# Keeping the instruction scheduler's time by a simulated timeline of the engines instead of plain estimates


## The chip, the cores and the metric

The kernel runs on one core of one Trainium2 chip. The metric is the device time of one execution in microseconds (us). The engines named below are TensorE (PE, matrix products), VectorE (DVE), ScalarE (ACT), GpSimd (POOL, which does nothing but fills of constants in this kernel) and SyncE (SP), whose queue issues most DMA transfers. Each engine runs its own list of instructions in the order in which the list was written, and an instruction that waits holds up those behind it in its list.

## The reference, cut to what matters

Two blocks of a language model are chained over 512 tokens of width 1024, all in fp32. The first block has a mixer of gated convolution and block-sparse attention, a gated MLP, a mixer with a linear recurrence, and a second MLP. The second block puts 16 learned tokens ahead of the 512 and has two layers, each with a hybrid mixer and a convolution-gated MLP:

```
def hybrid_mixer(...):
    proj = n @ w_in
    aq, ak, av, az, aa, ab, bq, bk, bv, iq, ik, iw = jnp.split(proj, SPLIT_POINTS, axis=-1)
    o_a = gated_deltanet(aq, ak, av, az, aa, ab, conv_a, a_log, dt_bias, a_out_norm)
    o_b = dsa_attention(bq, bk, bv, iq, ik, iw, q_norm, k_norm, kidx_norm, cos_a, sin_a, cos_i, sin_i)
    gates = jax.nn.sigmoid(n @ w_gate + b_gate).reshape(Bsz, T, 2, D)
    y = gates[:, :, 0] * (o_a @ w_branch_a) + gates[:, :, 1] * (o_b @ w_branch_b)
    return y @ w_out

def gated_deltanet(...):
    ...
    lhs = m + jnp.eye(CHUNK, dtype=f32)
    sol = lax.linalg.triangular_solve(lhs, rhs, left_side=True, lower=True, unit_diagonal=True)
    ...
    def step(S, inp):
        v_new = u_c - jnp.einsum('bhcd,bhde->bhce', w_c, S)
        o = (jnp.einsum('bhcd,bhde->bhce', q_c * jnp.exp(g_c)[..., None], S)
             + jnp.einsum('bhcs,bhse->bhce', qk_c, v_new))
        S = S * jnp.exp(g_last) + ...
        return S, o
```

The attention (`dsa_attention`) scores every key for every query with a small indexer, keeps the best keys and attends to those. The delta net solves a unit lower triangular system for each chunk of 128 tokens and carries a state `S` from chunk to chunk.

## The kernel before

**Products.** Every large matrix product runs in split precision: weight and activation are each cut into a high and a low part, and `products` (matmuls in line 146) forms high·high, high·low and low·high for each of 8 blocks of 128 rows, in two column halves. One block of 128 output columns is so 48 matmuls of 258 or 264 columns. Each weight block is loaded by an SP transfer into `wraw` (3 buffers), cast to its high part `whi` on ACT (line 97), and the low part `wlo` is subtracted on DVE (line 98; two buffers each). Product tiles `mm` in PSUM have two buffers, and so has each of the tags `a`, `b` and `c` that all smaller matmuls write to.

**The mixer of the second block** (`mixer_2`, run for layer 0 from about 1120 us and for layer 1 from about 2040 us) is where small work is laid between products. It goes through these stages: the norm's broadcast of the inverse root to all partitions (matmul of line 279, of a diagonal that DVE writes in line 266); products for queries and keys with the sums of squares (line 765) and the indexer's scores (lines 876 and 877); 12 products for the delta net's convolved inputs, with the selection of keys and the attention (lines 1014 to 1070) beside them; and 4 + 16 products for `z` and the gates (`w_gate`), with the delta net's matrices (`dn_keys`, `dn_prep`) beside them. Closures in the list `fill` are run between products in program order, one list entry per product:

```
            for k, p in enumerate(prods):
                if k < len(steps):
                    self.fill.append((1, lambda k=k: [f() for f in steps[k]]))
                p()
```

**The triangular solve** (`dn_solve`) is a chain over engines and transfers. The last `dn_prep` matmuls (line 1186) and DVE products (line 1188) give the matrices; SP stores them to DRAM (`md`, line 1191) and loads them in another layout (`U`, line 1220); 31 steps of two DVE instructions follow (lines 1226 and 1228), a copy (line 1229), SP stores and loads again (`xz`, lines 1232 to 1240), and then four rounds of small matmuls join the blocks: `pair1` (line 1250) to `pair4` (line 1283), each with a copy by ACT behind it. After that the state recurrence runs over 5 tiles of tokens: `dn_read` (line 1330), `dn_u` (line 1338), `dn_write` (line 1348) and `dn_out` (lines 1360 and 1364). The products with `w_branch_b` (line 1444, 8 blocks of 24 matmuls) don't need the delta net, those with `w_branch_a` do.

**What sets the order.** The kernel is written in one program order; the tile framework's scheduler then runs that program in a model of time and puts on each engine's list, whenever that engine is free in the model, the waiting instruction with the best priority. Its notion of how long things take thus decides which instruction stands ahead of which on an engine. The lists are fixed before the run. The line that the change touches is 1679, where the framework's context is opened around `body`, which writes the whole kernel.

## Time and profile before

| what | value |
|---|---|
| median of 3 runs | 2968.08 us (2965.66 to 2968.27) |
| profiled execution | 2972.7 us, of which the span of its profile 2970.9 us |
| PE busy in the span | 97% |
| mean granted TensorE clock | 0.974 of full |

The span runs from the first to the last profiled instruction. PE, PEld, DVE, ACT and POOL are engines (PEld is TensorE's loading of weights, which runs beside its matmuls). PEclk is the clock that TensorE was granted; its two levels are 2.4 GHz (1.00) and 1.2 GHz (0.50), and a value between the two is a mix over the stretch.

### The profile page before, as it was taken

How to read it: one execution, taken by the hardware profiler on the slowest of the kernel's cores; microseconds unless marked ns; L12 is line 12 of the kernel's file. 1: busy time of each engine (PE TensorE's matmuls, PEld its weight loads, DVE VectorE, ACT ScalarE, POOL GpSimd, SP SyncE). 2: the span in 40 equal slices, each digit the busy share in tenths (PEclk: the TensorE clock that was granted, in tenths of full speed). 3: DMA queues.
4: the chain of work that ended last, by engine and by line, in shares of the span. 5: the costliest groups of instructions: out<-in, count | busy, mean ns of one | idle time of the engine just before them, and what ended most of it. 6: DMA issues, size and time to landing. Idle time of an engine off the chain costs nothing.

```text
span 2970.9 us, 44580 instructions
## 1 busy us (share of the span) xinstructions
PE 2878.1 (97%) x18009; PEld 2521.7 (85%) x18009; DVE 1856.1 (62%) x3462; ACT 1047.0 (35%) x1939; POOL 14.2 (0%) x117
## 2 busy tenths in 40 slices
PE   7999999999999999998999999999999999999999
PEld 5767888876788887888999999999788999998897
DVE  7886535458653557698757554555788757565553
ACT  3444212245321233353633332223444634322222
POOL 0000000000000000000000000000000000000000
PEclk9999999999999999898999999999998999999999
DMA  4213333332333333121355232324221354332333
GB/s 124 63 32 120 92 100 92 94 98 71 93 94 98 93 99 111 54 65 51 102 137 154 83 89 86 93 84 122 57 65 43 86 141 116 109 90 85 103 88 90
DMA packets 509860, 272.23 MB, mean 92 GB/s; under 512 B 40112, under 2 KB 494918, under 8 KB 509398
## 3 DMA queue, kind: packets, MB, share of 16 engines
q1 hardware_dynamic: 493520, 245.24, 29.2%
q10 hardware_dynamic: 16134, 24.14, 2.5%
q8 instruction: 142, 2.33, 0.3%
q14 instruction: 64, 0.52, 0.1%
HBM read 249.11 MB, written 20.23 MB: 91 GB/s over the span
## 4 chain that ended last, share of the span: by engine, by line
PE 87%; DVE 8%; DMA 2%; ACT 2%; issue 1%; SPq 0%; ACTq 0%; DVEq 0%
PE mm L146 74%; PE mm L1444 2%; DVE wlo L98 1%; PE b L1065 1%; PE b L765 1%; PE a L393 1%; PE a L877 1%; PE c L418 1%; PE a L1022 1%; PE b L1062 1%; DVE ac L704 1%; DVE m L994 1%; DVE ac L966 1%; DVE selw L996 0%; PE a L876 0%
## 5 line engine op out<-in xcount | busy, mean ns | idle before, releaser
L97 ACT CAST whi<-wraw 128x1024 fp32r<-128x1024 f32 (+1 forms) x472 | 458.3, 971 | 1412.1 <-PE mm L146 1179.9
L146 PE MATMUL mm<-xh,whi 128*128 128x264 f32 (+2 forms) x3376 | 898.4, 323 | 15.4 <-ACT whi L97 6.4
L146 PE MATMUL mm<-xh,wlo 128*128 128x264 f32 (+2 forms) x3376 | 892.4, 322 | 11.6 <-DVE wlo L98 11.6
L146 PE MATMUL mm<-xl,whi 128*128 128x264 f32 (+2 forms) x3376 | 893.0, 322 | 0.0
L98 DVE TENSOR_TENSOR wlo<-wraw,whi 128x1024 fp32r<-128x1024 f32 (+1 forms) x472 | 529.2, 1121 | 423.1 <-ACT whi L97 413.2
L146 PEld LDWEIGHTS mm<-xh,whi 128*128 128x128 f32 x3376 | 564.8, 191 | 71.2 <-ACT whi L97 7.2
L146 PEld LDWEIGHTS mm<-xh,wlo 128*128 128x128 f32 x3376 | 566.6, 191 | 65.4 <-DVE wlo L98 16.7
L146 PEld LDWEIGHTS mm<-xl,whi 128*128 128x128 f32 x3376 | 563.1, 191 | 50.8 <-issue 7.0
L146 PE MATMUL mm<-hh,whi 128*128 128x512 f32 (+1 forms) x1040 | 340.7, 355 | 0.0
L146 PE MATMUL mm<-hh,wlo 128*128 128x512 f32 (+1 forms) x1040 | 340.4, 355 | 0.0
L146 PE MATMUL mm<-hl,whi 128*128 128x512 f32 (+1 forms) x1040 | 339.5, 354 | 0.0
L146 PEld LDWEIGHTS mm<-hh,wlo 128*128 128x128 f32 x1040 | 184.0, 188 | 27.7
L146 PEld LDWEIGHTS mm<-hl,whi 128*128 128x128 f32 x1040 | 183.8, 188 | 27.8
L146 PEld LDWEIGHTS mm<-hh,whi 128*128 128x128 f32 x1040 | 184.0, 188 | 26.5
L502 DVE TENSOR_TENSOR down<-mm,r 128x512 f32<-128x512 f32 x32 | 22.1, 692 | 106.7 <-PE mm L146 106.7
L361 DVE SCALAR_TENSOR_TENSOR val<-z,cw,val 128x512 f32<-128x512 f32 x120 | 84.8, 746 | 0.5
L1496 DVE TENSOR_TENSOR fx<-mm,rbc 128x528 f32<-128x528 f32 (+1 forms) x44 | 30.7, 702 | 81.6 <-PE mm L146 81.6
L1509 DVE TENSOR_TENSOR fc<-fc,mm 128x528 f32<-128x528 f32 (+1 forms) x44 | 30.6, 696 | 76.5 <-PE mm L146 76.5
L146 PE MATMUL mm<-qkv,whi 128*128 128x264 f32 (+1 forms) x384 | 67.4, 284 | 0.0
L1501 DVE SCALAR_TENSOR_TENSOR fc<-fx,vcols,fc 128x528 f32<-128x528 f32 (+1 forms) x88 | 66.2, 758 | 1.4
L1097 DVE TENSOR_TENSOR ac<-mm,rbc 128x528 f32<-128x528 f32 (+1 forms) x32 | 22.4, 700 | 70.3 <-PE mm L146 70.1
L1444 PE MATMUL mm<-xh,whi 128*128 128x264 f32 (+1 forms) x256 | 54.7, 295 | 7.3 <-DVE ax L1458 6.1
(538 smaller groups left out, 3327.5 us busy)
## 6 DMA issues: line engine op xcount, KB each, us to landing
wraw<-in_w_up SPq DMA_DIRECT2D x152, 512.0 KB, 4.0
wraw<-in_w_down SPq DMA_DIRECT2D x96, 512.0 KB, 4.3
wraw<-in_w_in SPq DMA_DIRECT2D x52, 512.0 KB, 3.9
wraw<-in_w_gate SPq DMA_DIRECT2D x32, 512.0 KB, 4.2
wraw<-in_ab_w_in SPq DMA_DIRECT2D x20, 512.0 KB, 3.7
wraw<-in_c_w_in SPq DMA_DIRECT2D x16, 512.0 KB, 3.9
wraw<-in_w_out SPq DMA_DIRECT2D x16, 512.0 KB, 5.4
wraw<-in_w_down SPq DMA_DIRECT2D x32, 192.0 KB, 2.6
```

The source lines that it names most:

```text
L97: self.S.copy(hi[:, :n], raw[:, :n])
L98: self.V.tensor_tensor(lo[:, :n], raw[:, :n], hi[:, :n].bitcast(F32), op=ALU.subtract)
L146: ins = self.PE.matmul(o, lhsT=wt[:, k % chunk, :], rhs=xt[:, t0:t1], start=n == 0, stop=n == 3 * kb - 1)
L361: V.scalar_tensor_tensor(cacc[b], z[b][:, j:j + S], w, cacc[b], op0=ALU.mult, op1=ALU.add)
L393: PE.matmul(ps[:, :W], lhsT=qk[p][r0:r0 + 64, P * i:P * i + P], rhs=qk[4 + p][r0:r0 + 64, :W], start=True, stop=True)
L418: PE.matmul(po[:, 64 * j:64 * j + 64], lhsT=pts[:, P * c:P * c + P], rhs=vt[c][:, h:h + 64], start=c == 0, stop=c == i)
L704: self.V.tensor_tensor(t[o], raw[i], tab[1][i], op=ALU.mult)
L765: PE.matmul(p5[:n, i:i + 1], lhsT=q[:, t0:t0 + n], rhs=self.ones[:, 0:1], start=True, stop=True)
L1444: PE.matmul(o, lhsT=wt[:, k, :], rhs=xt[:, m0 + t0:m0 + t1], start=k == 0 and j == 0, stop=k == 3 and j == 2)
L1496: V.tensor_tensor(self.v3(x[:, 2:2 + TG], TG), ps, self.v3(self.rbc, TG), op=ALU.mult)
L1501: V.scalar_tensor_tensor(c, x[:, d + j:TG + j], w(j), c, op0=ALU.mult, op1=ALU.add)
L1509: V.tensor_tensor(self.v3(c, TD), self.v3(c, TD), ps, op=ALU.mult)
```

## The change

The scheduler's clock is changed: it takes the time of instructions from a simulated timeline of the engines and no longer from plain per-instruction estimates. No instruction's computation is changed. GpSimd does memsets alone before and after.

```
-    with tile.TileContext(nc) as tc:
+    with tile.TileContext(nc, schedule_with_timeline_sim=True) as tc:
         body(tc, a, out)
```

The MLPs, the output products and nearly all of the first block's recurrence mixer keep their order. Instructions move in the first block's first mixer and in both hybrid mixers. In the rows below, a name is a tile and a number its instance: `mm` a product's tile, `xh`, `xl` and `whi`, `wlo` the parts of activation and weight, `a` and `b` small PSUM tiles, and the sizes at the end are of the output; x2 stands for two column halves.

Where layer 0's hybrid mixer begins, PE's list of before has the norm's broadcast (line 279) after 4 matmuls of the second product:

```order
L146 MATMUL mm_8390<-xl_1428_7544,whi_8392 128x264 x2
L146 MATMUL mm_8390<-xh_1427_7543,wlo_8393 128x264 x2
L146 MATMUL mm_8462<-xh_1413_7529,whi_8464 128x264 x2
L146 MATMUL mm_8462<-xl_1414_7530,whi_8464 128x264 x2
L279 MATMUL a_8355<-diag_8314,ones 128x512
L285 MATMUL a_8359<-diagm_8316,ones 128x16
L810 MATMUL mm_8539<-xh_1413_7529,whi_8533 80x264 x2
L810 MATMUL mm_8539<-xl_1414_7530,whi_8533 80x264 x2
L279 MATMUL a_8445<-diag_8375,ones 128x512
```

After the change the same broadcast (`a_8355`) stands in a later product:

```order
L146 MATMUL mm_8706<-xh_1421_7537,wlo_8709 128x264 x2
L146 MATMUL mm_8706<-xh_1423_7539,whi_8708 128x264 x2
L146 MATMUL mm_8706<-xl_1424_7540,whi_8708 128x264 x2
L279 MATMUL a_8355<-diag_8314,ones 128x512
L285 MATMUL a_8359<-diagm_8316,ones 128x16
L146 MATMUL mm_8706<-xh_1423_7539,wlo_8709 128x264 x2
L146 MATMUL mm_8706<-xh_1425_7541,whi_8708 128x264 x2
L146 MATMUL mm_8706<-xl_1426_7542,whi_8708 128x264 x2
```

The broadcast, and with it what waits for it, has moved behind 174 further product matmuls.

At the first small matmuls behind the triangular solve of layer 0 (`pair1`, line 1250), PE's list of before goes on with gate products (`mm_12235` is one of `w_gate`):

```order
L146 MATMUL mm_12128<-xh_1427_7543,whi_12130 128x264 x2
L146 MATMUL mm_12128<-xl_1428_7544,whi_12130 128x264 x2
L146 MATMUL mm_12128<-xh_1427_7543,wlo_12131 128x264 x2
L1250 MATMUL a_12183<-qkv_2099_11637,dec_11088 32x32
L1250 MATMUL b_12195<-qkv_2099_11637,dec_11198 32x32
L146 MATMUL mm_12235<-xh_1413_7529,whi_12237 128x264 x2
L146 MATMUL mm_12235<-xl_1414_7530,whi_12237 128x264 x2
L146 MATMUL mm_12235<-xh_1413_7529,wlo_12238 128x264 x2
```

After the change `pair1` stands behind all gate products and behind the first two `w_branch_b` products (line 1444):

```order
L1444 MATMUL mm_13064<-xh_2222_12625,whi_13057 128x264 x2
L1444 MATMUL mm_13029<-xl_2223_12626,whi_13022 128x264 x2
L1444 MATMUL mm_13029<-xh_2222_12625,wlo_13023 128x264 x2
L1444 MATMUL mm_13064<-xl_2223_12626,whi_13057 128x264 x2
L1444 MATMUL mm_13064<-xh_2222_12625,wlo_13058 128x264 x2
L1250 MATMUL a_12183<-qkv_2099_11637,dec_11088 32x32
L1250 MATMUL b_12195<-qkv_2099_11637,dec_11198 32x32
L1250 MATMUL a_12183<-qkv_2099_11637,dec_11088 32x32 x7
```

So the four products of gates that stood behind `pair1` and the two branch products now stand ahead of it. At the same time the last full `dn_prep` matmuls (line 1186) have moved 7 products later. Between these and `pair1` there are now 251 product matmuls where there were 403 (layer 1: 202 where there were 428).

From the last round (`pair4`, line 1283) to the recurrence's start in layer 0, PE's list of before has a product of 48 matmuls next, of which the first rows are shown:

```order
L146 MATMUL mm_12469<-xh_1427_7543,whi_12471 128x264 x2
L146 MATMUL mm_12469<-xl_1428_7544,whi_12471 128x264 x2
L146 MATMUL mm_12469<-xh_1427_7543,wlo_12472 128x264 x2
L1283 MATMUL a_12524<-XT_11629,t_2186_12438 64x64 x4
L1283 MATMUL b_12530<-XT_11631,t_2188_12445 64x64 x4
L1283 MATMUL a_12536<-XT_11633,t_2190_12452 64x64 x4
L1283 MATMUL b_12542<-XT_11635,t_2192_12459 64x64 x4
L146 MATMUL mm_12552<-xh_1413_7529,whi_12554 128x264 x2
L146 MATMUL mm_12552<-xl_1414_7530,whi_12554 128x264 x2
L146 MATMUL mm_12552<-xh_1413_7529,wlo_12555 128x264 x2
```

After the change rounds and recurrence follow on one another:

```order
L1276 MATMUL a_12437<-qkv_2099_11637,dec_11088 64x64 x4
L1276 MATMUL b_12444<-qkv_2099_11637,dec_11198 64x64 x4
L1276 MATMUL a_12451<-qkv_2100_11640,dec_11307 64x64 x4
L1276 MATMUL b_12458<-qkv_2100_11640,dec_11416 64x64 x4
L1283 MATMUL a_12524<-XT_11629,t_2186_12438 64x64 x4
L1283 MATMUL b_12530<-XT_11631,t_2188_12445 64x64 x4
L1283 MATMUL a_12536<-XT_11633,t_2190_12452 64x64 x4
L1283 MATMUL b_12542<-XT_11635,t_2192_12459 64x64 x4
L1338 MATMUL a_12635<-sacc_2083_11506,XTm_11705 16x128 x4
L1348 MATMUL a_12642<-sacc_2083_11506,sacc_10811 128x128 x4
L1364 MATMUL b_12649<-sacc_2083_11506,qkTm_11536 16x128 x4
L1330 MATMUL a_12679<-x_2225_12641,qkv_1719_9328 128x128
```

There is no product matmul left between `pair1` and the third `w_branch_b` product, where there were 144 between `pair1` and `pair4` and 96 from there to the third branch product, in each layer. On DVE, evictions and weight subtractions of the later products move along with PE's rows; on SP the `md` stores move behind all but one of the gate weights' loads, and the `xz` stores behind seven `w_branch_b` loads.

In the first block's first mixer the attention heads are spread later, so that the last two and a half pairs of heads have 15 product matmuls beside them, where before only the last pair had few.

## Rows read from the trace of the kernel before

**Rows 1.** The page: the span and the engines' busy time

```profile
span 2970.9 us, 44580 instructions
PE 2878.1 (97%) x18009; PEld 2521.7 (85%) x18009; DVE 1856.1 (62%) x3462; ACT 1047.0 (35%) x1939; POOL 14.2 (0%) x117
```

**Rows 2.** Waits of PE: who waited for whom, us in total, times, longest

```profile
PE a L279 <- DVE diag L266: 9.3, 4, 4.9
...
PE a L1250 <- DMA qkv<-xz: 5.0, 4, 2.2
```

**Rows 3.** Windows: stretch, length, busy us (instructions) by engine, clock, DMA share, GB/s

```profile
1120.00:1452.00 332.00, 313.32 (x2101) 278.50 (x2100) 256.51 (x599) 151.55 (x358) 3.34 (x28) 0.91 0.24 69
2040.00:2361.00 321.00, 304.74 (x2162) 275.91 (x2162) 249.43 (x577) 149.61 (x349) 3.14 (x25) 0.94 0.24 65
```

**Rows 4.** Windows of both layers ahead of the solve, at PE's low places

```profile
1160.00:1180.00 20.00, 13.68 (x61) 10.00 (x61) 19.45 (x36) 5.48 (x10) 0.21 (x2) 0.66 0.28 82
1350.00:1380.00 30.00, 23.86 (x117) 20.09 (x115) 23.36 (x54) 11.29 (x28) 0.00 (x0) 0.66 0.13 36
1210.00:1240.00 30.00, 29.93 (x110) 21.08 (x110) 14.45 (x28) 11.12 (x23) 0.50 (x2) 0.66 0.11 30
2080.00:2100.00 20.00, 16.08 (x117) 14.20 (x116) 19.46 (x30) 8.68 (x14) 0.00 (x0) 1.00 0.20 53
2260.00:2290.00 30.00, 23.86 (x115) 19.94 (x114) 23.34 (x53) 10.72 (x25) 0.00 (x0) 0.66 0.12 36
2130.00:2170.00 40.00, 39.56 (x181) 29.23 (x181) 22.44 (x39) 15.88 (x29) 0.65 (x3) 0.74 0.10 27
```

**Rows 5.** Windows: a stretch of products alone

```profile
2050.00:2060.00 10.00, 10.00 (x84) 10.00 (x83) 5.04 (x8) 2.84 (x4) 0.00 (x0) 1.00 0.65 183
```

**Rows 6.** Timeline of PE in layer 0: start us, us, instruction, idle before

```profile
1451.68 1.05 PE L1186 MATMUL b<-qkv 128*128 128x128 f32 x8
...
1507.41 0.22 PE L1250 MATMUL a<-qkv,dec 32*32 32x32 f32 x2 [0.53 <-DMA qkv<-xz]
...
1541.46 1.04 PE L1338 MATMUL a<-sacc,XTm 16*16 16x128 f32 x8
...
1571.20 0.49 PE L1444 MATMUL mm<-xh,whi 128*128 128x264 f32 x2
```

**Rows 7.** Timeline of DVE in layer 0's solve

```profile
1452.77 1.13 DVE L1188 SCALAR_TENSOR_TENSOR dec<-b,dmj,dec 128x128 f32<-128x128 f32 x4
...
1464.52 0.17 DVE L1226 TENSOR_TENSOR x<-qkv,x 128x31 f32<-128x31 f32 x1
...
1492.80 0.64 DVE L1229 COPY x<-x 128x512 f32<-128x512 f32 x1
```

**Rows 8.** Windows: 10 us of layer 0's recurrence

```profile
1560.00:1570.00 10.00, 8.43 (x66) 7.64 (x66) 9.90 (x45) 6.09 (x27) 0.00 (x0) 1.00 0.00 1
```

**Rows 9.** Timeline of PE in layer 1

```profile
2360.70 1.16 PE L1186 MATMUL b<-qkv 128*128 128x128 f32 x8
...
2420.07 0.22 PE L1250 MATMUL a<-qkv,dec 32*32 32x32 f32 x2 [1.12 <-DMA qkv<-xz]
...
2456.38 1.04 PE L1338 MATMUL a<-sacc,XTm 16*16 16x128 f32 x8
...
2486.09 0.48 PE L1444 MATMUL mm<-xh,whi 128*128 128x258 f32 x2
```

**Rows 10.** Timeline of DVE in layer 1's solve

```profile
2362.72 1.12 DVE L1188 SCALAR_TENSOR_TENSOR dec<-b,dmj,dec 128x128 f32<-128x128 f32 x4
...
2375.70 0.18 DVE L1226 TENSOR_TENSOR x<-qkv,x 128x31 f32<-128x31 f32 x1
...
2405.09 0.64 DVE L1229 COPY x<-x 128x512 f32<-128x512 f32 x1
```

**Rows 11.** Windows: the first mixer's last heads, and the recurrence mixer

```profile
190.00:240.00 50.00, 41.58 (x185) 29.84 (x184) 39.55 (x81) 22.55 (x57) 0.00 (x0) 0.86 0.14 40
...
600.00:760.00 160.00, 152.99 (x614) 115.61 (x613) 118.55 (x185) 79.00 (x107) 0.74 (x8) 0.98 0.29 83
```

## Prediction

> **What bounds the kernel now.** I read the page first, then the waits, then windows over the places where the lists differ, then the timeline through the solve. The page says that PE is busy for 97% of 2970.9 us while DVE is busy for 62% [rows 1]: the kernel is bound by products, and an order can only win what PE loses in idle time and at the lower clock, or lose more there. The windows say where that is: from 1120 to 1452 us (layer 0, up to the last `dn_prep` matmuls) PE is busy for 313.32 of 332 us at a mean clock of 0.91, and from 2040 to 2361 us (layer 1) for 304.74 of 321 us at 0.94 [rows 3]. Idle time and missing clock together are 18.7 + 313.3 × 0.09 = 46.9 us in layer 0 and 16.3 + 304.7 × 0.06 = 34.6 us in layer 1, 81.5 us in all. That is what better order ahead of the solve could give at most. Stretches of products alone run at full clock with 84 matmuls in 10 us, 0.119 us each [rows 5].
>
> Where PE is low, DVE is often full: 19.45 of 20 us in 1160 to 1180 and 19.46 of 20 in 2080 to 2100 [rows 4]. There PE's list holds an instruction that waits for DVE while products stand behind it. The wait for the norm's diagonal (line 279) is one such, 9.3 us in four waits [rows 2].
>
> **The change part by part.** No instruction's work is altered, so the sum has only stalls in it, and products that move from a place where they covered a chain to a place where they cover another.
>
> *The solve, uncovered.* In layer 0 the last full `dn_prep` matmuls start at 1451.68 and the third `w_branch_b` product at 1571.20, with `pair1` at 1507.41 and the recurrence's first `dn_u` at 1541.46 [rows 6]: 119.5 us. Between these marks PE's list loses 403 − 251 = 152 product matmuls ahead of `pair1`, 144 between `pair1` and `pair4` and 96 behind it, 392 in all, or 46.6 us at 0.119. They now stand ahead of line 1186. If PE remained the bound in this stretch, it would take 119.5 − 46.6 = 72.9 us. But the chain does not get shorter. Its parts: from the matmuls to the end of line 1188, 1452.77 + 1.13 − 1451.68 = 2.2 us; from there over the `md` stores, the `U` loads and DVE's work in between to the first step, 10.6 us; the steps, 1464.52 to 1492.80, 28.3 us [rows 7]. In DVE's new list the work between the first step and the copy is some 3 us more by the durations of before (28.6 instead of 25.7 us, evictions and weight subtractions that moved along), so I take 30. From the copy to `pair1` it is 14.6 us of copy, stores and loads. From `pair1` to `dn_u` it was 34.1 us with 192 product matmuls (22.8 us) in it; bare, the rounds can't be under 11 us, and they hold waits for the loads and ACT's copies that the products covered, so 13. The recurrence took 29.7 us with 48 matmuls (5.7 us) among it; DVE was busy for 9.90 of 10 us there [rows 8], so what can go lies between 0 and 5.7 us, and nearer to 0 by that row: 27. Sum: 2.2 + 10.6 + 30 + 14.6 + 13 + 27 = 97.4 us, 24.5 more than 72.9. The reader should see PE stand for over 20 us ahead of `pair1`: it has 251 × 0.119 = 30 us of products against 57 us of chain. On SP the `md` stores and `U` loads stand behind one more weight load at most that waits for a buffer; this I cost at nothing, since the loads behind them are what PE no longer needs at once. If that weight's buffer came free late, each us would be a us of the chain.
>
> Layer 1 goes the same way: 2486.09 − 2360.70 = 125.4 us [rows 9]; displaced are 428 − 202 = 226, 144 and 96 matmuls, 466 or 55.5 us, leaving 69.9. The chain has 3.1 + 11.9 us to the first step at 2375.70, 29.4 us of steps (31 with 1.6 more as in layer 0), 15.0 from the copy to `pair1` [rows 9, 10], then 13 and 27 as in layer 0: 101 us, 31.1 more.
>
> *The clock behind that wait.* In 1350 to 1380 PE stood idle for 6.1 us and then worked at a mean of 0.66 of its clock, which cost 23.86 × 0.34 = 8.1 us more [rows 4]. So after a stand of over 20 us the rounds start at 1.2 GHz. Rounds and recurrence are bound by ACT, loads and DVE for more than half, so I charge 3.5 us a layer out of 0 to 8.1, 7 in all. The Trainium skill (TensorE: Matmul & The Clock Gate, Part 1, "HAM oscillation") says that work in short bursts with waits between starts every burst at the lower clock; the case above agrees for one burst after a wait. By that rule the whole of rounds and recurrence would run at 1.2 GHz, and the sum would be that of the second rival below.
>
> The three terms give +24.5 + 31.1 + 7 = +62.6 us.
>
> *What comes back ahead of the solve.* The places where PE loses most in rows 4 are 1160 to 1180 (6.3 idle, 4.7 by clock: 11.0 us), 1350 to 1380 (14.3 us), 2080 to 2100 (3.9 us) and 2260 to 2290 (14.3 us), 43.5 us in all. At each, DVE's chain is late and PE's list now has product matmuls where the waiting instruction stood: the broadcast of line 279 is 174 matmuls (21 us) later in layer 0, and attention and `dn_keys` some seven products later. So I take the whole 43.5 us. The score stages lose at the clock rather than by idling: 10.2 us in 1210 to 1240 and 10.7 us in 2130 to 2170 [rows 4]; there small scores stand alone in the new list as in the old, even in a thicker clump. Of these 20.9 us and of the 17.1 us scattered over the rest I take a quarter, 9.5 us. The term is −53.0 us, between −21.8 (half of the 43.5, if DVE at over 19 of 20 us stays the bound there, and nothing else) and −81.5.
>
> *The first block.* From 190 to 240 us PE is busy for 41.58 of 50 us at 0.86 of its clock, which loses 14.2 us [rows 11]. The new list has the last two and a half pairs of heads nearly bare instead of one, and more products spread ahead; between −5 and +14, I take +3. In the recurrence mixer, 600 to 760, PE idles for 7.0 us [rows 11]; few instructions move, and I take +1 of −3 to +3.
>
> **The sum.** 62.6 − 53.0 + 4 = +13.6 us. The profiled execution took 2972.7 us, 4.6 more than the median 2968.1 of the runs shown; the changed kernel's would take 2986.3, and its median, with the same distance, 2981.7 us.
>
> **Rivals.**
> *First, faster: DVE gets far enough behind PE's list that nothing ahead of the solve waits.* Then all of the 81.5 us come back, scores too, and the sum is 62.6 − 81.5 + 4 = −15 us: 2953 us. For it speaks that every stall there is PE standing in order behind DVE or ACT, and that PE's list has 46.6 and 55.5 us more products to lay in between. Against it, DVE is busy for 19.4 of 20 us at these places [rows 4], and PE can't run ahead further than two PSUM buffers let it. It decides for faster once more than 67 us come back.
> *Second, much slower: the clock stays low from `pair1` to the third branch product.* PE's own work there is about 22 us a layer at full clock (the 40 us of rounds and recurrence above, less waits). At half clock each matmul in the chain takes twice its time; where DVE is not the bound I put 15 us a layer, 30 for both instead of 7. The sum is then 62.6 + 23 − 53.0 + 4 = +36.6 us: 3005 us. For it: the work there is short bursts between waits. Against it: in before the recurrence ran at 1.00 with DVE at 9.90 of 10 [rows 8].
> *Third, no change that can be measured:* the products moved ahead fill as much as they uncover, 66 us instead of 53: 2968 us. Nothing in the rows prefers it; it lies between forecast and first rival.
>
> **How the numbers follow.** About 0.2% (6 us) is what a measurement of this kernel can tell from no change. I give 0.36 to the forecast (its own range 2975 to 2996), 0.29 to the first rival, 0.20 to the second and 0.15 to the third. So faster 0.29, same 0.15, slower 0.56. For the range: the first rival with the low bounds of the tail (rounds 11 us, recurrence 24, no lower clock: 17 us less) would end near 2936, the second with only 44 us coming back ahead of the solve near 3014. Leaving out the outer tenths, I give 2941 to 3012 us.
>
> **What the changed profile would show.** PE idle for 20 to 35 us ahead of `pair1` in both layers, with the wait for the `xz` loads (line 1250), 5.0 us in all before [rows 2], grown to over 40 us; the distance from the last line 1186 to the third line 1444 product near 97 and 101 us; clock at 1.2 GHz for a stretch behind the wait; no wait of over 2 us at line 279 in layer 0; and less idle time from 1350 to 1380 and from 2260 to 2290. The prediction is wrong if the stages ahead of the solve shrink by over 67 us, if the solve's chain is shorter when DVE has less beside it, or if other engines, freed, start the chain much sooner.

## The result and the profile after

The changed kernel took 3003.99 us (median of 4 runs, 2996.30 to 3007.97) against 2968.18 us before (4 runs, 2965.66 to 2971.88) on the same chip: 1.0117 times, 95% interval 1.0090 to 1.0143. It is slower by 35.8 us. The profiled execution was the fastest of its four, 2996.3 us, and that of the kernel before (2972.7 us) lay 4.5 us over its median, so the two spans differ by 23.5 us and the rows explain two thirds of the difference.

The page of the changed kernel, its span and busy times, against [rows 1]: PE is busy for 11.6 us less in a span that is 23.5 us longer.

```profile
span 2994.4 us, 44642 instructions
## 1 busy us (share of the span) xinstructions
PE 2866.5 (96%) x18009; PEld 2524.0 (84%) x18009; DVE 1863.4 (62%) x3462; ACT 1043.2 (35%) x1939; POOL 13.7 (0%) x117
```

PE's waits in the changed kernel, against [rows 2] (who waited for whom, us in total, times, longest):

```profile
PE a L1250 <- DMA qkv<-xz: 49.0, 6, 22.1
PE a L279 <- DVE diag L266: 7.7, 3, 3.8
PE a L855 <- DVE ikr L849: 6.5, 1, 6.5
PE mm L146 <- DVE gg L584: 6.3, 1, 6.3
```

The wait at `pair1` (line 1250) has grown from 5.0 to 49.0 us. The prediction did not name the last two waits: 6.5 us in layer 0's hybrid mixer (line 855), and 6.3 us in the first block's recurrence mixer.

Windows of the changed kernel over the stretches that answer to [rows 3], and behind them from the last full `dn_prep` matmuls to `pair1` and from `pair1` to the third `w_branch_b` product, layer 0 and layer 1:

```profile
1130.00:1482.00 352.00, 342.73 (x2487) 315.16 (x2486) 271.70 (x611) 165.41 (x374) 3.20 (x28) 0.96 0.30 86
2056.00:2411.00 355.00, 351.23 (x2627) 327.93 (x2626) 270.04 (x600) 165.81 (x374) 2.88 (x25) 0.96 0.29 82
1482.00:1537.00 55.00, 37.37 (x364) 35.50 (x362) 37.31 (x114) 13.08 (x24) 0.00 (x0) 0.88 0.50 122
1537.00:1586.00 49.00, 38.57 (x419) 33.98 (x417) 26.91 (x98) 16.88 (x74) 0.00 (x0) 0.72 0.14 28
2411.00:2464.00 53.00, 30.93 (x313) 29.12 (x311) 33.95 (x105) 11.31 (x22) 0.00 (x0) 0.83 0.48 115
2464.00:2512.00 48.00, 38.55 (x420) 34.28 (x418) 26.39 (x97) 16.64 (x73) 0.00 (x0) 0.69 0.14 28
```

Ahead of the solve PE is now idle for 9.3 and 3.8 us where it was idle for 18.7 and 16.3 us [rows 3]. From there to `pair1` it is idle for 17.6 and 22.1 us, and in rounds and recurrence its clock is 0.72 and 0.69.

The timeline of the changed kernel in layer 0, PE first and then DVE, against [rows 6, 7]:

```profile
1482.34 1.06 PE L1186 MATMUL b<-qkv 128*128 128x128 f32 x8
...
1536.77 0.31 PE L1250 MATMUL a<-qkv,dec 32*32 32x32 f32 x2 [17.63 <-DMA qkv<-xz]
...
1554.30 1.88 PE L1338 MATMUL a<-sacc,XTm 16*16 16x128 f32 x8
...
1585.53 0.51 PE L1444 MATMUL mm<-xh,whi 128*128 128x264 f32 x2 [0.36 <-DVE qkv L1452]
```

```profile
1492.62 0.19 DVE L1226 TENSOR_TENSOR x<-qkv,x 128x31 f32<-128x31 f32 x1 [1.93 <-DMA qkv<-md]
...
1527.06 0.59 DVE L1229 COPY x<-x 128x512 f32<-128x512 f32 x1
```

To see where time goes, I matched the same DVE and ACT instructions in both traces and took the difference of their starts (the median within 8 us). Against the kernel before, the changed one is 6.2 us ahead behind the first block's first mixer (340 us), 9.9 us late behind its recurrence mixer (780 to 1110 us), 16.1 us late behind layer 0's hybrid mixer, 25.4 us late behind that of layer 1, and 23.9 us late near the end. So in this execution the first mixer gives 6.2 us, the recurrence mixer takes 16.1 us, and the two hybrid mixers take 6.2 and 9.3 us.

### The profile page after: what moved, and what is told of

The parts are those of the page before. It is cut to its first block, busy times and chain, and to the rows that moved or that the text cites. A ratio compares the mean times of both kernels' runs of the same rounds, so it can differ in the third digit from the quotient of the medians.

```text
span 2994.4 us, 44642 instructions
## 1 busy us (share of the span) xinstructions
PE 2866.5 (96%) x18009; PEld 2524.0 (84%) x18009; DVE 1863.4 (62%) x3462; ACT 1043.2 (35%) x1939; POOL 13.7 (0%) x117
## 4 chain that ended last, share of the span: by engine, by line
PE 91%; DVE 5%; DMA 2%; ACT 1%; issue 1%; SPq 0%; ACTq 0%; DVEq 0%
PE mm L146 78%; PE mm L1444 2%; PE b L765 1%; PE a L877 1%; DVE wlo L98 1%; PE b L1065 1%; PE a L393 1%; PE a L1022 1%; PE a L876 1%; PE c L418 1%; DMA ax<-gd 1%; PE b L1062 1%; ACT whi L97 0%; PE a L1348 0%; DMA qkv<-xz 0%
## 5 line engine op out<-in xcount | busy, mean ns | idle before, releaser
L502 DVE TENSOR_TENSOR down<-mm,r 128x512 f32<-128x512 f32 x32 | 22.1, 692 | 106.8 <-PE mm L146 106.8
L1503 ACT ACTIVATE fx<-fc 128x528 f32<-128x528 f32 (+1 forms) x44 | 28.1, 639 | 88.8 <-DVE fc L1501 88.7
```

## The experiments

The theory to be tested: the hybrid mixers lose because the solve's chain stands bare, the first block loses in the recurrence mixer. The rivals: the wait at `pair1` is not the cost, or product matmuls are worth the same wherever they stand. All ratios are to the kernel before on the same chip.

**The scans kept apart.** Between 705 and 725 us the changed kernel's DVE is full while PE works at low clock and waits. The window, then DVE's timeline and PE's wait behind it:

```profile
705.00:725.00 20.00, 9.72 (x26) 7.50 (x27) 19.97 (x25) 3.87 (x6) 0.00 (x0) 0.67 0.23 66
```

```profile
715.16 2.34 DVE L577 TENSOR_TENSOR_SCAN xc<-at,xc 128x512 f32<-128x512 f32 x2
717.41 0.68 DVE L590 SCALAR_TENSOR_TENSOR gg<-gu,gg 128x512 f32<-128x512 f32 x1
717.99 2.34 DVE L577 TENSOR_TENSOR_SCAN xc<-at,xc 128x512 f32<-128x512 f32 x2
720.24 0.68 DVE L211 TENSOR_TENSOR yl<-gg,wt 128x512 fp32r<-128x512 f32 x1
720.83 0.70 DVE L591 TENSOR_TENSOR gg<-gg,xc 128x512 f32<-128x512 f32 x1
721.43 1.23 DVE L98 TENSOR_TENSOR wlo<-wraw,whi 128x1024 fp32r<-128x1024 f32 x1
722.56 0.70 DVE L584 TENSOR_TENSOR gg<-mm,rbc 128x512 f32<-128x512 f32 x1
```

```profile
723.40 0.76 PE L146 MATMUL mm<-xh,whi 128*128 128x512 f32 x1 [6.35 <-DVE gg L584]
```

The scans of all eight blocks (lines 575 to 577) run before the third gate block's eviction (line 584); both product buffers are full until then. The edit:

```
-                V.tensor_tensor(g, ps, self.rbc, op=ALU.mult)
+                gi = V.tensor_tensor(g, ps, self.rbc, op=ALU.mult)
...
-                scan(b)
+                with self.tc.issue_after(gi.ins):
+                    scan(b)
```

> The changed kernel, with one pin: in the recurrence mixer, the DVE instructions of scan block b (three of them) are put behind the eviction of gate block b (line 584) on DVE's list. Theory: the changed kernel loses 16 us between 620 and 780 us because its list for DVE has the scans of all eight blocks in one clump ahead of the third gate eviction, so that PE waits for a product tile; with the pin, PE's idle time there (18.1 us with the lower clock 27 us) falls to about the 10 us of the kernel before and the time falls by 13 to 17 us against the changed kernel, to some 2987 us median (3004 less 16). Rival: the loss there comes from PE's list or from late weights, and the clump only fills DVE's waiting time; then the stretch keeps its 16 us and the time is 3004.

Measured: 2997.03 us, ratio 1.0120 (1.0082 to 1.0158). The same window with the pin, and the evictions with scans between them:

```profile
703.00:723.00 20.00, 19.07 (x76) 15.00 (x75) 19.21 (x28) 8.67 (x13) 0.00 (x0) 0.91 0.36 106
```

```profile
707.15 0.68 DVE L584 TENSOR_TENSOR gg<-mm,rbc 128x512 f32<-128x512 f32 x1
...
710.16 1.22 DVE L577 TENSOR_TENSOR_SCAN xc<-at,xc 128x512 f32<-128x512 f32 x1
...
713.76 0.68 DVE L584 TENSOR_TENSOR gg<-mm,rbc 128x512 f32<-128x512 f32 x1
```

The recurrence mixer loses 7.3 us instead of 16.1: the clump is worth 8.8 us, little more than half of what I expected. The medians do not show it (1.0120 with the pin, 1.0117 without, with intervals wider than 9 us); the profiles do. In all six that have the clump the mixer loses 16.0 to 17.5 us, in all four that have the pin 7.2 to 8.6. Part of the rest stands ahead of the scans: at the norm's broadcast (line 279) PE waits 3.4 us with and without the pin, where it did not wait before. Before, 24 product matmuls stood between line 255 and that broadcast, now 9.

**The cover put back.** The first pin on the hybrid mixers holds the last 12 of the 20 z and gate products behind the last full `dn_prep` matmul.

```
-                    PE.matmul(pkk[:, h, :], ...)
+                    prep[i] = PE.matmul(pkk[:, h, :], ...)
...
-                p()
+                with self.tc.issue_after(prep[3].ins) if k >= 8 else ExitStack():
+                    p()
```

> The changed kernel, with one pin: from the ninth of the 20 z and gate products on, a product's matmuls stand behind the last full dn_prep matmul on PE's list. Between that matmul and pair1 there are then 442 product matmuls in layer 0 and 456 in layer 1 (changed kernel 251 and 202, before 403 and 428), between pair1 and pair4 108 and 116, and 74 and 52 behind. Theory A (two separate terms): the 60.8 us that the uncovered solve costs in both layers go, and PE's wait ahead of pair1 with them (49.0 us of waits at line 1250 fall under 8 us); the 47 us won ahead of the solve came half from better places of waiting instructions and stay by half, so both mixers together take 20 to 25 us less than in the kernel before, and with the recurrence mixer's 16 and the first mixer's -6 the time is about 2955 to 2960 us. Theory B (the same products can cover only once): what the pins give back behind the solve is lost ahead of it, where PE waits for DVE again; both mixers take what they take in the kernel before within 8 us, and the time is 2970 to 2985 us. Theory C (the wait at pair1 is not the cost): no gain, 3004 us.

Measured: 3014.73 us, ratio 1.0165 (1.0127 to 1.0202), the slowest of all and slower than any of the three theories gave: the wait at `pair1` went, but another took its place. PE's waits, one of them in PE's timeline with what DVE did until it ended, and windows of the stretch around it and of the chain:

```profile
PE a L1022 <- DVE s L1026: 18.8, 4, 9.6
```

```profile
1435.34 3.90 PE L1022 MATMUL a<-kT,qT 128*128 128x264 f32 x8 [8.09 <-DVE s L1026]
```

```profile
1434.39 0.43 DVE L1008 TENSOR_SCALAR score<-selw 128x512 f32<-128x512 f32 x1
1434.85 0.77 DVE L1026 TENSOR_TENSOR s<-a,score 128x264 f32<-128x264 f32 x2
```

```profile
1420.00:1470.00 50.00, 36.22 (x175) 29.21 (x175) 25.18 (x56) 21.20 (x81) 0.00 (x0) 0.70 0.10 32
...
1482.00:1542.00 60.00, 59.24 (x542) 57.36 (x540) 42.24 (x120) 18.45 (x33) 0.00 (x0) 1.00 0.57 141
```

The chain to `pair1` is covered again (PE busy for 59.24 of 60 us at full clock). But ahead of it PE has used up its products by 1427 us, and then waits for the last attention units: DVE takes their scores (line 1026) only when it has ended the selection of keys (line 1008). Ahead of the solve, 373 matmuls fewer in layer 0 (44 us) shortened the stretch by only 16 us.

**The chain shortened, in both kernels.** One edit, in the changed kernel and in the one before; it leaves out the last 16 of the solve's 31 steps in each layer:

```
-                for j in range(BS - 1):
+                for j in range(15):
```

> The changed kernel with the last 16 of the 31 steps of the solve left out in both layers (the inverse's blocks are then unfinished; all else is computed on them); the lists of PE are otherwise the same. Theory: PE stands for the chain's whole length, so every us taken out of the chain shortens the kernel: the steps left out took 9.6 us of DVE in each layer, in a stretch of 15.5 and 11.2 us: 19 to 27 us less than the changed kernel, and PE's wait at pair1 shorter by 9 to 14 us a layer. Rival: PE's wait at pair1 is a wait for the transfers behind the steps or for DVE's other work; then the time falls by less than 8 us.

> The kernel before with the same 16 steps left out in both layers. Theory: there products cover the chain, which ends with only 5.0 us of waits at pair1 in both layers, so at most 5 us can be won: 2963 to 2968 us. Rival: the steps cost DVE time that other work needs, in either kernel; then about 19 us are won here too.

Measured in the changed kernel: 2976.65 us, ratio 1.0046 (1.0031 to 1.0062); the unshortened one has 1.0117 and 1.0120, so 0.7%, some 21 us, came back. PE's waits at `pair1`, layer 0 and layer 1:

```profile
1537.59 0.31 PE L1250 MATMUL a<-qkv,dec 32*32 32x32 f32 x2 [8.11 <-DMA qkv<-xz]
...
2449.90 0.28 PE L1250 MATMUL a<-qkv,dec 32*32 32x32 f32 x2 [14.53 <-DMA qkv<-xz]
```

They are 9.5 and 7.5 us shorter; for layer 1 I had expected at least 9. From the last `dn_prep` matmuls to the last branch matmul it takes 139.0 and 137.4 us instead of 152.6 and 149.4. In the kernel before: 2956.29 us, ratio 0.9975 (0.9958 to 0.9992), 7 us, and the same distance falls from 169.4 and 175.1 to 164.1 and 170.0 us, 5 us a layer. So the covered chain costs some, somewhat more than the 5 us that I allowed in all, and the bare one more than twice as much: the theory of the wait stands.

**The changed kernel again.**

> The changed kernel once more, to see it beside the others on one chip. Theory: in the first block's first mixer the same list has two outcomes, seen in the profiles so far: TensorE's clock comes back to 1.00 within the weak stretch near 200 us (place of the mixer's end -6 and -7 us against the kernel before) or stays at 0.50 to 0.67 until 220 us (+4 and +9 us). So the median lies 1.009 to 1.014 times the kernel before, the single runs spread over 8 to 16 us, and a profile shows one of the two outcomes. Rival: the spread comes from all stages alike; then the first mixer's place is neither.

Measured: 3001.76 us (2992.74 to 3004.74), ratio 1.0120 (1.0095 to 1.0146); the first mixer's end stands at -3.6 us, near the earlier of the two expected places. Windows of the weak stretch of the first mixer in this run:

```profile
180.00:195.00 15.00, 15.00 (x48) 8.33 (x47) 11.39 (x27) 7.77 (x26) 0.00 (x0) 0.60 0.00 1
195.00:210.00 15.00, 14.13 (x93) 10.54 (x94) 7.56 (x22) 10.74 (x39) 0.00 (x0) 1.00 0.00 1
```

And the same windows of the run with the new first block alone (the last experiment of this section), whose lists are the same there:

```profile
180.00:195.00 15.00, 14.88 (x38) 8.38 (x38) 10.14 (x24) 6.98 (x25) 0.00 (x0) 0.50 0.00 1
195.00:210.00 15.00, 15.00 (x56) 11.35 (x56) 3.78 (x10) 5.13 (x21) 0.00 (x0) 0.50 0.00 0
```

The new list of the first mixer was profiled ten times in all. In four the clock was 1.00 from 195 to 210 us and the mixer's end stood between -7.0 and -2.6 us; in six it was 0.50 there and the end stood between +3.6 and +8.6 us. The old list, profiled three more times, ended between -0.1 and +1.6 us. The list is the same each time; what decides between the two outcomes is not in these rows.

**DVE relieved.** The weight subtractions of the 20 z and gate products go to GpSimd, in the changed kernel and in the one before.

```
-        self.V.tensor_tensor(lo[:, :n], raw[:, :n], hi[:, :n].bitcast(F32), op=ALU.subtract)
+        getattr(self, "lo", self.V).tensor_tensor(lo[:, :n], raw[:, :n], hi[:, :n].bitcast(F32), op=ALU.subtract)
...
+            self.lo = self.G
             for k, p in enumerate(prods):
```

> The changed kernel, with the weight subtraction (wlo, line 98) of the 20 z and gate products of each hybrid mixer on GpSimd instead of DVE, 1.2 us of DVE work each, 24 us a layer. PE's list then has 358 and 357 product matmuls between the last full dn_prep matmuls and pair1 (changed kernel 251 and 202) and none behind. Theory (ahead of the solve DVE's list sets the time, and every product moved ahead of the solve brings its 1.9 us of DVE work with it): the last full dn_prep matmuls come 15 to 25 us earlier from each layer's start than in the changed kernel (358 and 361 us there), with the rest of the chain as long, and the time falls by 30 to 50 us against the changed kernel, to 2955 to 2975 us. Rival 1 (ahead of the solve PE or the clock sets the time): the distance stays within 8 us but for the products that are no longer in it, and the time is 2985 to 3004 us. Rival 2 (GpSimd's subtraction is slow or holds DVE up): PE waits for wlo, and the time is over 3004 us.

> The kernel before, with the same 20 weight subtractions a layer on GpSimd. Its list has 387 and 384 product matmuls from the last full dn_prep matmuls to pair1 (403 and 428 before), the rest as before. Theory (DVE sets the time of the attention stage there too): the last full dn_prep matmuls come 8 to 20 us earlier in each layer, less the time of the matmuls that moved ahead, and the time falls by 10 to 30 us: 2935 to 2955 us. Rival 1: no change within 6 us, since PE is 97% busy. Rival 2 (GpSimd slow or in DVE's way): slower by over 6 us.

> The changed kernel with both edits: the subtractions on GpSimd and the pin that keeps the scans of the recurrence mixer apart. Theory: the gains add, 7 to 11 us less than with the subtractions alone. Rival: the scan's pin only moved a wait and is worth nothing here, within 4 us.

Measured: 2983.50 us on the changed kernel, ratio 1.0061 (1.0040 to 1.0081), 18 us less than without; 2999.57 us on the one before, ratio 1.0120 (1.0096 to 1.0145), 37 us more; with the scans' pin 2979.33 us, ratio 1.0053 (1.0038 to 1.0068). Ahead of the solve the changed kernel takes 345 and 341 us instead of 358 and 361, which is what the 107 and 155 matmuls that left the stretch are worth (12.7 and 18.4 us), and PE's idle time there is the same 9.3 and 3.8 us, though DVE is busy there for 12 and 10 us less. So in that list products set the time ahead of the solve, not DVE: rival 1, for that stretch. Both theories that expected a faster kernel from DVE's relief missed. What the edit won came from the cover: 358 matmuls ahead of `pair1`, and PE's waits there fell to 22.9 us. The kernel before, whose chain was covered, only paid the price: in its layer 0 the solve's steps take 29.7 us of DVE's time instead of 19.7. DVE's and GpSimd's timelines show how, here of the changed kernel with this edit:

```profile
1502.67 2.54 DVE L1226 TENSOR_TENSOR x<-qkv,x 128x207 f32<-128x207 f32 x1
1510.69 2.49 DVE L1226 TENSOR_TENSOR x<-qkv,x 128x255 f32<-128x255 f32 x1
```

```profile
1502.59 2.38 POOL L98 TENSOR_TENSOR wlo<-wraw,whi 128x1024 fp32r<-128x1024 f32 x1 [4.28 <-ACT whi L97]
1510.48 2.42 POOL L98 TENSOR_TENSOR wlo<-wraw,whi 128x1024 fp32r<-128x1024 f32 x1 [5.50 <-ACT whi L97]
```

A solve instruction of about 0.4 us that starts just after GpSimd's subtraction takes 2.5 us and ends 0.2 to 0.3 us behind it. The scans' pin took 9 us off the recurrence mixer again; its 4 us in the medians are within their intervals.

**Fewer products pinned**, 8 and 10 of the 20, with the scans' pin (`k >= 12` and `k >= 10` in the edit above).

> The changed kernel with the scan's pin and with the last 8 of the 20 z and gate products of each hybrid mixer behind the last full dn_prep matmul on PE's list: 432 product matmuls between it and pair1 in both layers, none between pair1 and the third branch product. Theory (ahead of the solve PE needs only as many products as last until DVE's chain is through, some 340 us; those left over are worth most ahead of pair1): the stretch ahead takes 337 to 345 us a layer (changed kernel 358 and 361, less 181 and 230 matmuls at 0.119), the chain to pair1 55 to 58 us without PE idle, rounds and recurrence 43 to 48 us at a clock near 1.00 at the start, the rest 91 and 114 us; so layer 0 takes 526 to 542 us (545 in the kernel before, 551 changed) and layer 1 about 15 less than in the kernel before. With 7 us lost in the recurrence mixer the time is 2940 to 2965 us, at least as fast as the kernel before. Rival 1 (PE runs dry ahead of the solve again, as with 12 products pinned): a wait at line 1022 of over 5 us and 350 us or more ahead; 2975 to 2995 us. Rival 2 (the clock falls in rounds and recurrence whatever stands ahead of pair1): 11 us a layer are lost there at 0.70 and the time is 2960 to 2975 us.

> The same with the last 10 products behind the dn_prep matmul: 434 and 455 matmuls to pair1, 94 and 73 between pair1 and pair4, none behind. Theory: PE runs dry ahead of the solve for a few us (a wait at line 1022 of 3 to 6 us), rounds are covered, so that the sum lies between those of 8 and of 12 pinned products: 2950 to 2985 us. Rival: the rounds' cover is worth more than the wait ahead costs, and this is faster than with 8 pinned products by over 5 us.

Measured: 2986.96 us, ratio 1.0078 (1.0060 to 1.0095), and 2987.57 us, ratio 1.0079 (1.0060 to 1.0097). Windows with 8 pinned, the chain and then rounds and recurrence:

```profile
1475.00:1537.00 62.00, 58.53 (x540) 56.56 (x540) 43.63 (x123) 20.10 (x36) 0.00 (x0) 1.00 0.52 135
1537.00:1586.00 49.00, 36.50 (x414) 32.47 (x415) 26.71 (x97) 17.09 (x72) 0.00 (x0) 0.72 0.22 54
```

Both forecasts missed (2940 to 2965 and 2950 to 2985 us). With 8 pinned, the clock was that of rival 2: PE came at full clock to `pair1`, and the bare rounds and recurrence still ran at 0.72; but its 2960 to 2975 us did not come. The time was that of rival 1, without its wait at line 1022. What failed is the stretch ahead: 21.5 and 27.4 us of products left it, and it became 10.2 and 19.7 us shorter. The stretches of both layers in us, from the same instruction ahead of the mixer to the last full `dn_prep` matmul, to `pair1`, to the third branch product, and to the same instruction in the following MLP:

| kernel | layer 0 | layer 1 |
|---|---|---|
| before | 337.3 + 55.1 + 63.8 + 88.8 = 545.0 | 326.5 + 58.6 + 66.0 + 113.9 = 565.0 |
| changed | 358.1 + 53.8 + 48.7 + 90.5 = 551.1 | 360.7 + 52.0 + 47.7 + 113.9 = 574.3 |
| 12 pinned | 342.4 + 60.4 + 60.1 + 97.9 = 560.8 | 333.6 + 62.1 + 56.2 + 119.2 = 571.1 |
| 10 pinned, scans | 348.8 + 59.0 + 48.6 + 91.4 = 547.8 | 336.6 + 62.1 + 46.8 + 114.2 = 559.7 |
| 8 pinned, scans | 347.9 + 61.6 + 49.0 + 94.4 = 552.9 | 341.0 + 62.4 + 46.8 + 114.2 = 564.4 |

No version that computes the whole beat the kernel before. In layer 0, what a pinned product wins behind the last `dn_prep` matmul is about lost ahead of it; in layer 1, 8 or 10 pinned win back the 9 us. Differences under some 5 us can't be read from this table, which has one execution of each kernel: in the profile of the last experiment the second block's old lists took 540.2 and 561.7 us, not 545.0 and 565.0, and the row of 10 pinned comes from an execution of 2971.9 us, 15.7 us under its median. With 12 pinned, 7.4 and 5.3 us of the loss lie behind the third branch product, where the lists have as many product matmuls as the changed kernel's; why is open.

**Each half alone.** All instructions of the first block on PE, DVE, ACT and SP were pinned to the other kernel's lists, so that one kernel has the old first block with the new second block and one the reverse.

```
         body(tc, a, out)
+        pin(tc, nc)
...
+            if last:
+                tc.add_manual_dep(ins[f"I-{n}"], last, info, reason="pin")
```

> The lists of the kernel before in the whole first block (PE, DVE, ACT and SP pinned to it instruction by instruction), the lists of the changed kernel in the second block. Theory: the parts add. The hybrid mixers take 6 to 9 us and 4 to 9 us more in the changed kernel's profiles than in the profile before, so the time is 12 to 18 us over the kernel before on the same chip, 2976 to 2984 us, and the single runs spread less than those of the changed kernel (8 to 16 us), since the first mixer's two outcomes are out. Rival: the mixers cost most of the 36 to 39 us by which the medians differ, and the profiles caught them in a good execution: over 25 us, 2990 us or more.

> The other half: the lists of the changed kernel in the first block, those of the kernel before in the second. Theory: 16 us from the recurrence mixer, where the scans stand in a clump, and between -7 and +9 us from the first mixer: 12 to 25 us over the kernel before, 2976 to 2990 us. Rival: the first block costs under 8 us.

Measured: the new second block alone 2983.90 us, ratio 1.0067 (1.0052 to 1.0082), 18.5 us; the new first block alone 2984.19 us, ratio 1.0068 (1.0053 to 1.0082), 18.7 us. PE's longest waits, of the one and of the other:

```profile
PE a L1250 <- DMA qkv<-xz: 48.5, 6, 21.7
```

```profile
PE mm L146 <- DVE gg L584: 7.8, 1, 7.8
```

Together 37.2 us, which is the whole difference (35.8 and 39.0 us on the two chips where the changed kernel ran): the halves add within their intervals (some 4 us each), and the first block costs as much as the second.

## Why the prediction was right, and which terms were off

The forecast of slower held: 3004.0 us, 22 us over the 2981.7 of the sum and within its range, but outside the forecast's own 2975 to 2996 us. That it is the second rival's 3005 us is chance: the solve, which should have made that difference, came out as the sum had it, and the first block made most of it.

*The solve, uncovered* (forecast +24.5, +31.1 and 7 for the clock, 62.6 in all). From the last `dn_prep` matmuls to the third branch product, the changed kernel takes 1585.53 - 1482.34 = 103.2 us in layer 0 and 100.4 in layer 1; against the 72.9 and 69.9 us that the displaced products would have left, that is +30.3 and +30.5, 60.8 us. The parts moved against each other in layer 0: to the first step 10.3 us (forecast 12.8), the steps 34.4 (30), copy to `pair1` 9.7 (14.6), rounds 17.5 (13), recurrence 31.2 (27). The last two hold the lower clock, 0.72 in their window in layer 0 and 0.69 in layer 1, which I had charged with 3.5 us a layer. Of the signs, the wait at line 1250 and the clock behind it came; PE's 17.6 us of idle time in layer 0 is under the 20 to 35 named. The shortened chain shows that this wait does cost time.

*What comes back ahead of the solve* (forecast -53). The stretch is 20.8 us longer in layer 0 and 34.2 in layer 1, with 46.6 and 55.5 us more of products in it: -25.8 and -21.3, 47.1 us. The size was right. PE's waits name part of it, of the kernel before and of the changed one:

```profile
PE b L765 <- ACT sqq L760: 12.9, 6, 4.9
```

```profile
PE b L765 <- ACT sqq L760: 2.1, 2, 1.0
```

The one wait that the forecast named is at line 279, where the kernel before waited 3.0 and 1.3 us in the two stretches; the sums of squares (line 765) cost 6.5 us in each. What I took the 47 us for was not quite right: the pins show that they aren't there without the products. Take them out of the stretch, and PE stands before the attention of line 1022 for 8.09 us at once. The two terms are two sides of one: products cover either DVE's chain ahead or the solve behind. With 12 of them put back, layer 0 took 9.7 us more than in the changed kernel and layer 1 3.2 us less.

*The first block* (forecast +4) is the term that was mis-sized: 9.9 us in the profile and 18.7 in the medians. "Few instructions move" was read from PE's list. In the recurrence mixer about a third of DVE's 199 instructions had changed places in its list, all scans ahead of an eviction that PE waits for, and the mixer lost 16.1 us where I had +1; the clump of scans is 8.8 us of that. In the first mixer, +3 lies between its two outcomes. With 16.1 in place of 1 the forecast would have been 2997 us.

*The rivals.* The first (all 81.5 us come back) did not come: 47 did. The second, the low clock from `pair1` to the third branch product, happened in part, and within the 60.8 us: in layer 0 the clock is at its lower level through the rounds and into the recurrence, and at its higher one from there on:

```profile
1537.00:1565.00 28.00, 22.52 (x300) 19.89 (x298) 7.79 (x22) 8.23 (x32) 0.00 (x0) 0.50 0.24 49
1565.00:1586.00 21.00, 16.05 (x121) 14.08 (x121) 19.12 (x77) 8.65 (x42) 0.00 (x0) 1.00 0.00 1
```

The Trainium skill (TensorE: Matmul & The Clock Gate, Part 1, "HAM oscillation") tells of a kernel in which every burst of matmuls behind a wait for a transfer starts at the lower clock. The trace agrees for the rounds, behind the wait of 17.63 us. It doesn't for the whole: in the second window PE still stands for up to 1.6 us between its matmuls, at 1.00.

The hybrid mixers cost 15.4 us in the changed kernel's profile against the one before, 22.9 us between the two profiles of the last experiment, and 18.5 us in the medians; one execution of each kernel does not fix them better.

## What to carry to other kernels

When a scheduler's clock is changed, compare the lists of every engine, the one that evicts products above all: behind a list of PE that hardly moved stood one of DVE that had, and that mixer lost 16.1 us, as much as both hybrid mixers together (15.4). Count product matmuls as a store that covers one of two chains, and ask which chain is left bare and whether PE's clock survives that. Where the profile and the medians differ, pin each half to the old lists and time it: the halves added up here to 37.2 us of 35.8 and 39.0.

## What the runs showed of the hardware

The same list had two outcomes in a weak stretch: with the clock at 1.00 or at 0.50 from 195 to 210 us, 6 to 16 us apart, four times and six. And a DVE instruction of about 0.4 us with two SBUF operands took 2.5 us when a GpSimd subtraction of 2.4 us had started 0.1 to 0.2 us ahead of it (the changed kernel with the subtractions on GpSimd). The Trainium skill (GPSIMD Engine Reference, 1. Specifications) says that GpSimd shares its SBUF interfaces with VectorE, with contention for instructions with two SBUF inputs; the trace agrees: the short instruction ended just behind the long one, while the 18 instructions MAX8 and MATCH_REPLACE8 of the same trace that started inside a subtraction took no longer than elsewhere.
